# Scan loads of a hybrid encoder layer: keys stored by scan step, gate rows loaded once for each direction

## The chip, the cores and the metric

The kernel runs on one NeuronCore of a Trainium2 chip. The metric is the device time of one execution in microseconds, lower is better. One core has five engines that run side by side, each through its own list of instructions in order: TensorE (PE), VectorE (DVE), ScalarE (ACT), GpSimd (POOL) and SyncE (SP). SP computes nothing here: it issues the transfers between the chip's memory (HBM) and the core's SBUF. The core's 16 DMA engines carry them out.

## The reference

One encoder layer on 2,048 tokens of width 1,024, all in float32. Three head groups read the same normalised input; their outputs go through one projection and are added to the residual. Then come cross attention to 256 memory tokens and a squared-ReLU MLP.

```python
h = rmsnorm(x, norm_mix_w[l])
(na_q, ..., gd_b, gd_a) = jnp.split(h @ w_in[l], IN_OFFSETS, axis=-1)
y_na = neighbourhood_attention(na_q, na_k, na_v, na_rel_bias[l])      # 6 heads of 64
y_ml = mlstm_mixer(...)            # 4 heads of 64, forwards and backwards
y_gd = gated_deltanet_mixer(...)   # 6 heads of 64, forwards and backwards
x = x + jnp.concatenate([y_na, y_ml, y_gd], axis=-1) @ w_out[l]
x = x + memory_cross_attention(rmsnorm(x, norm_xa_w[l]), rmsnorm(mem, norm_mem_w[l]), ...)
h = rmsnorm(x, norm_ffn_w[l])
x = x + jnp.square(jax.nn.relu(h @ w_ff1[l])) @ w_ff2[l]
```

The two recurrent groups cut the tokens into 32 chunks of 64 and carry a 64 x 64 state from chunk to chunk, once forwards and once backwards:

```python
# gated DeltaNet, one direction, chunk by chunk
def step(state, xs):
    u_c, w_c, a_c, qd_c, ks_c, gl_c = xs
    v_new = u_c - jnp.einsum('bhld,bhde->bhle', w_c, state)
    o = jnp.einsum('bhld,bhde->bhle', qd_c, state) + jnp.einsum('bhls,bhse->bhle', a_c, v_new)
    state = state * jnp.exp(gl_c)[..., None, None] + jnp.einsum('bhld,bhle->bhde', ks_c, v_new)
    return state, o
# mLSTM, one direction: c_prev, n_prev, m_prev come from such a scan too
m_t = jnp.maximum(jnp.max(dmat, axis=-1), inter)
s_intra = jnp.einsum('bhnld,bhnsd->bhnls', q, k) * jnp.exp(dmat - m_t[..., None])
a_inter = jnp.exp(inter - m_t)
num = a_inter[..., None] * (q @ c_prev) + s_intra @ v
```

## The kernel before

`mix` does the first half of the layer in three passes, `tail` the rest. **Pass A** projects the DeltaNet inputs in four blocks of 512 tokens, makes the gates, and for each token tile of 128 (`gram`) forms the products of keys and queries; `inv` inverts the triangular matrices. All that the scans need is written to scratch tensors in HBM: the inverses `w_d`, query products and state keys `sc_d`, decayed keys `kb_d`, values `v_d`, convolved queries `gd_c`, decay rows `g_st`.

**Pass B** runs the two scans, `gdn_scan` and `ml_scan`, side by side, 16 steps each. A step `m` does forward tile `m` and backward tile `15 - m` together: the forward direction lies in partitions 0 to 63 and the backward one in 64 to 127 (`CH`; `SR` is the other half for the state rows). A step has two halves (`i`), one chunk of 64 tokens each. In a half of `gdn_scan` matmuls (L680) make the new values, a copy on DVE (forward) and one on ACT (backward) bring them from PSUM to SBUF (L682), matmuls (L687) update the state, and two copies (L690) bring that back, so that the next half can begin; L694 and L696 make the output. Between the scans' instructions stands one piece per step of a list called `rest`: projections (L108) that do not depend on the scans.

Each step's inputs are loaded one step ahead by `load(m + 1)`. Of `gdn_scan`: `wp`, `sc` (two buffers each), `kb`, `ge`, `qe` (one buffer each). ACT takes the exponential of `ge` (L650), POOL multiplies `qe` with it (L653), PE multiplies `kb` with `wp` (L661). Of `ml_scan`: `mr_` (`r` in the code) and `msc` (`sc`) with two buffers, and `mkq`, `mqe`, `me` (`e`), `mge` with one. DVE subtracts `me` (L850), POOL masks it (L851), ACT takes its exponential (L852), and POOL multiplies `mqe` with `mge` (L871). Four loads of a step serve both directions with one transfer: `kb` (L641), `ge` (L649), `me` (L848), `mge` (L849). Their source is a slice of the form `[m:32 - m:31 - 2 * m]` of a tensor whose direction and tile are taken as one dimension; it has two elements, and behind it come 64 rows. In `ge`, `me` and `mge` the 64 rows are one row of HBM, read 64 times (`broadcast_to([2, 64, ...])`).

**Pass C** does the neighbourhood attention and the outputs of all heads; `tail` the output projection, cross attention and MLP.

The order of the instructions on each engine is set ahead by the framework's scheduler, which works from its own model of durations and from priorities; SP's list of transfers is part of that order. A load waits until its buffer is free. Each transfer that SP issues also waits for one of eight semaphores (`DMAHW0` to `DMAHW7`), which are used in turn.

Of the kernel before, what the change touches and what calls it, by code (L numbers as in the profile page):

```python
# [49 lines left out]
class Trunk:  # L50
# [61 lines left out]
    def mix(self, late):  # L112

        tc, nc, I, dr = self.tc, self.nc, self.I, self.dr
        dt = lambda name, shape: dr.tile(shape, F32, name=name)
        self.y_d = [dt(f"y_d{b}", [8, P, 512]) for b in range(4)]
        self.gd_c = dt("gd_c", [9, P, T])
        self.gate_d = dt("gate_d", [5, P, T])
        self.ho_d = dt("ho_d", [16, P, 2, 640])
        self.mlc_d = dt("mlc_d", [16, P, 4, P])  # L120
        self.mlv_d = dt("mlv_d", [16, P, 4, 65])
        self.nac_d = dt("nac_d", [6, P, T])
        self.nav_d = dt("nav_d", [T, 384])
        self.g_row = dt("g_row", [16, 2, 2, 6, 64])
        self.sc_d = dt("sc_d", [2, 16, 2, 64, 2, 6, 64])
        self.kb_d = dt("kb_d", [2, 16, 64, 2, 6, 64])
        self.g_st = dt("g_st", [2, 16, 2, 6, 64])
        self.v_d = dt("v_d", [16, 2, 64, 6, 64])
        self.x_d = dt("x_d", [384, 64, 64])
        self.w_d = [[dt(f"w_d{d}{g}", [64, 12 * (b - a), 64]) for g, (a, b) in enumerate(GROUPS)] for d in range(2)]  # L130
        self.wt_d = [dt(f"wt_d{d}", [192, 32, 32]) for d in range(2)]
        with ExitStack() as big:
            self.c = big.enter_context(self.pool("mixc", 1))
            c = self.c
            self.ind2 = self.load_const("ind2", [P, 2])
            self.gmask = self.load_const("gmask", [P, 2, 64])
            self.egl = c.tile([P, 4, 2, 2, 4, 6], F32, name="egl")
            self.rr = c.tile([P, 16, 12], F32, name="rr")
            self.gcm = c.tile([P, 2, 16, 4], F32, name="gcm")
            self.gtm = c.tile([P, 2, 16, 4], F32, name="gtm")  # L140
            self.cm = c.tile([P, 2, 16, 4], F32, name="cm")
            self.cmx = c.tile([P, 2, 16, 4], F32, name="cmx")
            self.wxx = c.tile([P, 2, 16, 4], F32, name="wxx")
            self.emt = c.tile([P, 2, 16, 4], F32, name="emt")
            self.rs = c.tile([P, 16], F32, name="rs")
            self.rp = big.enter_context(self.pool("rest", 2))
            self.np = big.enter_context(self.pool("nin", 1))
            rest = chain(self.ml_in((3, 2)), self.na_kv((3, 2)), self.renorm((0, 1)), self.na_kv((0, 1)), self.na_q((0, 1)), *([self.gdn_z((0, 1))] if ZB else []))
            self.pass_a(rest)
            self.pass_b(rest)  # L150
            for _ in rest:
                pass
            self.pass_c(late)
# [264 lines left out]
    def gram(self, t):  # L418

        nc, pool = self.nc, self.tp  # L420
# [3 lines left out]
        e = pool.tile([P, 2, 6, 64], F32, name="gr")  # L424
# [49 lines left out]
        for d in range(2):  # L474
            sc = pool.tile([P, 3, 6, 64], F32, name="sc")
            V.tensor_tensor(out=byp(sc[:, 0]), in0=gv[:, :, :, 0:64], in1=byp(e[:, d]), op=ALU.mult)
            V.tensor_tensor(out=sc[:, 1], in0=heads(kt), in1=col(kst[:, d]), op=ALU.mult)
            V.tensor_tensor(out=sc[:, 2], in0=heads(kt), in1=col(self.eg[:, t, d]), op=ALU.mult)
            nc.sync.dma_start(out=self.sc_d[d, t].rearrange("c s a h l -> (c s) (a h l)"), in_=sc[:, 0:2].rearrange("p a h l -> p (a h l)"))
            for c2 in range(2):  # L480
                nc.sync.dma_start(out=self.kb_d[d, t, :, c2], in_=sc[64 * c2:64 * c2 + 64, 2])

    def inv(self, g, dirs, late=False):

# [140 lines left out]
    def gdn_scan(self, pool):  # L625
# [4 lines left out]
        nc, dr = self.nc, self.dr  # L630
        V, G = nc.vector, nc.gpsimd
        CH = (slice(0, 64), slice(64, 128))
        SR = (slice(64, 128), slice(0, 64))

        def load(m):
            wp = pool.tile([P, 2, 2, 6, 64], F32, name="wp")
            sc = pool.tile([P, 2, 2, 3, 6, 64], F32, name="sc")
            kb = pool.tile([P, 2, 6, 64], F32, name="kb", bufs=1)
            ge = pool.tile([P, 2, 6, 64], F32, name="ge", bufs=1)
            qe = pool.tile([P, 6, P], F32, name="qe", bufs=1)  # L640
            nc.sync.dma_start(out=kb.rearrange("p c h l -> p (c h l)"), in_=self.kb_d.rearrange("d t s c h l -> (d t) s (c h l)")[m:32 - m:31 - 2 * m])  # L641
            for d in range(2):
                t = m if d == 0 else 15 - m
                g = next(g for g, (a, b) in enumerate(GROUPS) if a <= t < b)
                nc.sync.dma_start(out=wp[CH[d], d].rearrange("p c h l -> p (c h) l"), in_=self.w_d[d][g][:, 12 * (t - GROUPS[g][0]):12 * (t - GROUPS[g][0]) + 12])
                nc.sync.dma_start(out=sc[CH[d], d, :, 0:2].rearrange("p c a h l -> p c (a h l)"), in_=self.sc_d[d, t].rearrange("c s a h l -> s c (a h l)"))
                nc.sync.dma_start(out=sc[CH[d], d, :, 2].rearrange("p c h l -> p c (h l)"), in_=self.v_d[t].rearrange("c s h l -> s c (h l)"))
                nc.sync.dma_start(out=qe[SR[d]], in_=self.gd_c[0:3, :, P * t:P * t + P].rearrange("c (h e) l -> e (c h) l", h=2))
            nc.sync.dma_start(out=ge.rearrange("p c h l -> p (c h l)"), in_=self.g_st.rearrange("d t c h l -> (d t) (c h l)")[15 - m:17 + m:2 * m + 1, None].broadcast_to([2, 64, 768]))  # L649
            nc.scalar.activation(out=ge, in_=ge, func=AF.Exp)  # L650
            for d in range(2):
                t = m if d == 0 else 15 - m
                G.tensor_tensor(out=sc[SR[d], d, :, 0], in0=qe[SR[d]].rearrange("p h (c l) -> p c h l", c=2), in1=ge[SR[d]], op=ALU.mult)  # L653
                V.tensor_tensor(out=sc[SR[d], d, :, 1], in0=self.ident[SR[d], None, None, SR[d]].broadcast_to([64, 2, 6, 64]),
                                in1=self.egl[SR[d], t // 4, :, d, t % 4, :, None].broadcast_to([64, 2, 6, 64]), op=ALU.mult)
            for i in range(2):
                ps = self.sps.tile([P, 512], F32, name="pss")
                for h in range(6):
                    for d in range(2):
                        c2 = i if d == 0 else 1 - i  # L660
                        nc.tensor.matmul(out=ps[SR[d], 64 * h:64 * h + 64], lhsT=kb[CH[d], c2, h], rhs=wp[CH[d], d, c2, h], start=True, stop=True)  # L661
                for d in range(2):
                    c2 = i if d == 0 else 1 - i
                    nc.scalar.copy(out=wp[SR[d], d, c2], in_=ps[SR[d], :384].rearrange("p (h x) -> p h x", x=64))
            return wp, sc

        cur = load(0)
        for d in range(2):
            V.memset(cur[1][SR[d], d, d, 2], 0.0)
        evac = (V.tensor_copy, nc.scalar.copy)  # L670
        for m in range(16):
            nxt = load(m + 1) if m < 15 else None
            o = pool.tile([P, 2, 384], F32, name="o", bufs=1)
            wp, sc = cur
# [147 lines left out]
    def ml_scan(self, pool):  # L822
        tc, nc, dr = self.tc, self.nc, self.dr
        V, G = nc.vector, nc.gpsimd
        CH = (slice(0, 64), slice(64, 128))
        SR = (slice(64, 128), slice(0, 64))
# [7 lines left out]
        def load(m):  # L834

            sc = pool.tile([P, 2, 2, 2, 4, 64], F32, name="msc")
            r = pool.tile([P, 2, 2, 4, 65], F32, name="mr_")
            qe = pool.tile([P, 4, P], F32, name="mqe", bufs=1)
            ge = pool.tile([P, 4, P], F32, name="mge", bufs=1)
            kq = pool.tile([P, 2, 4, P], F32, name="mkq", bufs=1)  # L840
            e = pool.tile([P, 2, 4, 64], F32, name="me", bufs=1)
            for d in range(2):
                t = m if d == 0 else 15 - m
                nc.sync.dma_start(out=kq[:, d], in_=self.mlc_d[t])
                nc.sync.dma_start(out=r[CH[d], d].rearrange("p c h x -> p c (h x)"), in_=self.mlv_d[t].rearrange("(c s) h x -> s c (h x)", c=2))
                for a in range(2):
                    nc.sync.dma_start(out=qe[SR[d], a::2], in_=self.mlc_d[t, CH[a], 0:2])
            nc.sync.dma_start(out=e.rearrange("p c h l -> p (c h l)"), in_=self.mx_row.rearrange("d t c h l -> (d t) (c h l)")[m:32 - m:31 - 2 * m, None].broadcast_to([2, 64, 512]))  # L848
            nc.sync.dma_start(out=ge.rearrange("p h l -> p (h l)"), in_=self.ai_row.rearrange("d t h c l -> (d t) (h c l)")[15 - m:17 + m:2 * m + 1, None].broadcast_to([2, 64, 512]))  # L849
            V.tensor_tensor(out=e, in0=self.cmx[:, :, m, :, None].broadcast_to([P, 2, 4, 64]), in1=e, op=ALU.subtract)  # L850
            G.tensor_tensor(out=e, in0=e, in1=gm[:, None, None, :].broadcast_to([P, 2, 4, 64]), op=ALU.add)  # L851
            nc.scalar.activation(out=e, in_=e, func=AF.Exp)  # L852
# [16 lines left out]
            for d in range(2):  # L869
                t = m if d == 0 else 15 - m  # L870
# [3 lines left out]
            return sc, r  # L874

        cur = load(0)
        for d in range(2):
            V.memset(cur[1][SR[d], d, d], 0.0)
        evac = (V.tensor_copy, nc.scalar.copy)
        for m in range(16):  # L880
            nxt = load(m + 1) if m < 15 else None
            o = pool.tile([P, 2, 4, 64], F32, name="mo", bufs=1)
            sc, r = cur
# [528 lines left out]
```

## Time and profile before

| | |
|---|---|
| median of 2 runs | 4136.92 us (4133.67 to 4140.17) |
| the profiled execution | 4121.6 us |
| its span | 4119.8 us |
| PE busy | 3509.9 us, 85% of the span |
| DVE / ACT / POOL busy | 1794.2 / 1153.4 / 1583.3 us |
| moved by DMA | 466.17 MB, mean 113 GB/s |

The span is what the profiler recorded from the first instruction to the last; the execution's own time has 1.8 us around it. A busy share is an average over passes with different limits, so it is read stage by stage. Pass A lasts until about 840 us of the span, pass B until about 1,620, pass C until about 2,000; the rest is the tail, in which PE is busy almost without a break.

### The profile page before, as it was taken

How to read it: one execution, taken by the hardware profiler on the slowest of the kernel's cores; microseconds unless marked ns; L12 is line 12 of the kernel's file. 1: busy time of each engine (PE TensorE's matmuls, PEld its weight loads, DVE VectorE, ACT ScalarE, POOL GpSimd, SP SyncE). 2: the span in 40 equal slices, each digit the busy share in tenths (PEclk: the TensorE clock that was granted, in tenths of full speed). 3: DMA queues.
4: the chain of work that ended last, by engine and by line, in shares of the span. 5: the costliest groups of instructions: out<-in, count | busy, mean ns of one | idle time of the engine just before them, and what ended most of it. 6: DMA issues, size and time to landing. Idle time of an engine off the chain costs nothing.

```text
span 4119.8 us, 54195 instructions
## 1 busy us (share of the span) xinstructions
PE 3509.9 (85%) x21392; PEld 2805.2 (68%) x21392; DVE 1794.2 (44%) x3257; ACT 1153.4 (28%) x2015; POOL 1583.3 (38%) x947
## 2 busy tenths in 40 slices
PE   5878788865445556988999999999999999999998
PEld 4656666644334445655888888778888877888887
DVE  7697885513334343555543434532222244222224
ACT  3223232211111122444443333422211243221123
POOL 4444443622223223322544534433333354333333
PEclk9888888877767778988999999999999999999999
DMA  4638567554444445567423333321111132111112
GB/s 129 190 108 185 143 162 180 133 131 118 115 122 133 130 135 178 169 191 220 138 92 128 98 121 133 116 72 44 47 47 51 52 107 85 44 46 47 52 52 87
DMA packets 388902, 466.17 MB, mean 113 GB/s; under 512 B 152408, under 2 KB 280872, under 8 KB 385576
## 3 DMA queue, kind: packets, MB, share of 16 engines
q1 hardware_dynamic: 385032, 450.65, 37.5%
q0 software_dynamic: 3616, 12.06, 0.9%
q8 instruction: 169, 2.77, 0.3%
q14 instruction: 85, 0.70, 0.1%
HBM read 360.01 MB, written 102.60 MB: 112 GB/s over the span
## 4 chain that ended last, share of the span: by engine, by line
PE 48%; issue 1%; DVE 1%; ACT 1%; DMA 0%; POOL 0%; SPq 0%; POOLq 0%; DVEq 0%; ACTq 0%
PE psg L108 28%; PE psa L108 19%; PE psa L1192 0%; DMA wraw<-in_w_ff 0%; DVE nh L1017 0%; PE psm L99 0%; ACT whi L999 0%; DVE ss L1028 0%; PE psm L88 0%; DMA out_y<-nh 0%; POOL wlo L1001 0%; DVE xb L1263 0%; ACT acta L1149 0%; ACT acta L1018 0%; DVE nh L1263 0%
## 5 line engine op out<-in xcount | busy, mean ns | idle before, releaser
L1001 POOL TENSOR_TENSOR wlo<-wraw,whi 128x1024 fp32r<-128x1024 f32 (+2 forms) x401 | 838.8, 2093 | 1346.5 <-ACT whi L999 1306.3
L108 PE MATMUL psg<-acta,whi 128*128 128x512 f32 x3008 | 981.5, 407 | 41.6 <-ACT pad L297 22.4
L108 PE MATMUL psg<-actb,whi 128*128 128x512 f32 (+2 forms) x2752 | 862.2, 394 | 34.4 <-ACT pad L297 19.9
L999 ACT CAST whi<-wraw 128x1024 fp32r<-128x1024 f32 (+2 forms) x417 | 373.5, 896 | 1219.2 <-PE psa L108 557.3
L108 PEld LDWEIGHTS psg<-acta,whi 128*128 128x128 f32 x3008 | 579.9, 195 | 179.2 <-ACT pad L297 25.2
L108 PE MATMUL psa<-ht,whi 128*128 128x512 f32 x2048 | 638.5, 395 | 0.7 <-ACT whi L999 0.7
L108 PEld LDWEIGHTS psg<-actb,whi 128*128 128x128 f32 (+1 forms) x2752 | 520.9, 194 | 150.8 <-ACT pad L297 21.1
L108 PE MATMUL psg<-acta,wlo 128*128 128x512 f32 x1504 | 607.5, 405 | 9.1 <-POOL wlo L1001 9.1
L108 PE MATMUL psg<-actb,wlo 128*128 128x512 f32 (+2 forms) x1376 | 542.2, 395 | 19.3 <-POOL wlo L1001 19.3
L108 PEld LDWEIGHTS psa<-ht,whi 128*128 128x128 f32 x2048 | 384.1, 188 | 95.3 <-ACT whi L999 1.6
L108 PE MATMUL psa<-ht,wlo 128*128 128x512 f32 x1024 | 401.0, 396 | 0.5 <-POOL wlo L1001 0.5
L1241 DVE TENSOR_TENSOR fr<-fr 128x512 f32<-128x512 f32 x128 | 167.9, 1312 | 497.1 <-ACT fr L1240 497.1
L1254 DVE TENSOR_TENSOR xb<-psa,xb 128x512 f32<-128x512 f32 x256 | 175.6, 691 | 476.6 <-PE psa L108 476.6
L108 PEld LDWEIGHTS psg<-acta,wlo 128*128 128x128 f32 x1504 | 292.6, 195 | 77.8 <-POOL wlo L1001 12.6
L108 PEld LDWEIGHTS psg<-actb,wlo 128*128 128x128 f32 (+1 forms) x1376 | 266.6, 194 | 77.4 <-POOL wlo L1001 23.6
L1244 POOL TENSOR_TENSOR ht<-fr,ht 128x512 fp32r<-128x512 f32 x128 | 169.1, 1321 | 248.3 <-ACT ht L1243 247.0
L108 PEld LDWEIGHTS psa<-ht,wlo 128*128 128x128 f32 x1024 | 192.2, 188 | 47.2 <-POOL wlo L1001 1.7
L310 DVE SCALAR_TENSOR_TENSOR acc<-pad,vecs,acc 128x512 f32<-128x512 f32 (+2 forms) x144 | 151.8, 1057 | 1.1
L1028 DVE TENSOR_TENSOR ss<-ss,sqt 128x512 f32<-128x512 f32 (+1 forms) x91 | 120.3, 1322 | 51.5 <-ACT sqt L1027 48.4
L850 DVE TENSOR_TENSOR me<-cmx,me 128x512 f32<-128x512 f32 x16 | 11.1, 692 | 282.0 <-DMA me<-mx_row 199.9
L1243 ACT CAST ht<-fr 128x512 fp32r<-128x512 f32 x128 | 79.4, 621 | 180.3 <-DVE fr L1241 180.2
L680 PE MATMUL pss<-sc,wp 128*64 128x64 f32 x768 | 40.6, 251 | 98.7 <-ACT sc L690 69.7
(376 smaller groups left out, 4100.4 us busy)
## 6 DMA issues: line engine op xcount, KB each, us to landing
wraw<-in_w_ff SPq DMA_DIRECT2D x72, 512.0 KB
wraw<-in_w_ff SPq DMA_DIRECT2D x144, 256.0 KB
wraw<-in_w_gd SPq DMA_DIRECT2D x36, 512.0 KB
xt<-in_xT SPq DMA_DIRECT2D x16, 1024.0 KB
wraw<-in_w_out SPq DMA_DIRECT2D x32, 512.0 KB
wraw<-in_w_xq SPq DMA_DIRECT2D x32, 512.0 KB
wraw<-in_w_xo SPq DMA_DIRECT2D x32, 512.0 KB
sc_d<-sc SPq DMA_DIRECT2D x32, 384.0 KB
```

Source lines behind the costliest of these rows:

```text
L108: nc.tensor.matmul(out=out, lhsT=a(k), rhs=b(k), start=(i == 0), stop=(i == n - 1))
L310: V.scalar_tensor_tensor(out=acc[:, :n], in0=pad[:, p0 + j:p0 + j + n], scalar=cw(j), in1=acc[:, :n], op0=ALU.mult, op1=ALU.add)
L680: nc.tensor.matmul(out=ps[CH[d], 64 * h:64 * h + 64], lhsT=wp[:, d, cc[d], h], rhs=sc[:, d, cc[d], 2, h], start=True, stop=True)
L850: V.tensor_tensor(out=e, in0=self.cmx[:, :, m, :, None].broadcast_to([P, 2, 4, 64]), in1=e, op=ALU.subtract)
L999: nc.scalar.copy(out=hi, in_=raw)
L1001: (lo_eng or nc.gpsimd).tensor_tensor(out=lo, in0=raw, in1=hi.bitcast(F32), op=ALU.subtract)
L1028: nc.vector.tensor_tensor(out=ss, in0=ss, in1=sq, op=ALU.add)
L1241: V.tensor_tensor(out=r, in0=r, in1=r, op=ALU.mult)
L1243: S.copy(out=ht[:, 0], in_=r)
L1244: G.tensor_tensor(out=ht[:, 1], in0=r, in1=ht[:, 0].bitcast(F32), op=ALU.subtract)
L1254: V.tensor_tensor(out=xs[nb][:, j], in0=ps, in1=xs[nb][:, j], op=ALU.add)
```

## The change

`kb_d` gets the scan step as its first dimension: the key of backward tile `t` is stored under step `15 - t`, so that a step's load takes the two directions as 128 rows that follow each other. The loads of `ge`, `me` and `mge` become two transfers each, one for each direction, with 64 rows of the one source row. The values are the same, and so are the bytes; a step issues three transfers more.

```diff
-        self.kb_d = dt("kb_d", [2, 16, 64, 2, 6, 64])
+        self.kb_d = dt("kb_d", [16, 2, 64, 2, 6, 64])
...
             for c2 in range(2):
-                nc.sync.dma_start(out=self.kb_d[d, t, :, c2], in_=sc[64 * c2:64 * c2 + 64, 2])
+                nc.sync.dma_start(out=self.kb_d[15 - t if d else t, d, :, c2], in_=sc[64 * c2:64 * c2 + 64, 2])
...
-            nc.sync.dma_start(out=kb.rearrange("p c h l -> p (c h l)"), in_=self.kb_d.rearrange("d t s c h l -> (d t) s (c h l)")[m:32 - m:31 - 2 * m])
+            nc.sync.dma_start(out=kb.rearrange("p c h l -> p (c h l)"), in_=self.kb_d[m].rearrange("d s c h l -> (d s) (c h l)"))
...
-            nc.sync.dma_start(out=ge.rearrange("p c h l -> p (c h l)"), in_=self.g_st.rearrange("d t c h l -> (d t) (c h l)")[15 - m:17 + m:2 * m + 1, None].broadcast_to([2, 64, 768]))
+            for d in range(2):
+                nc.sync.dma_start(out=ge[SR[d]], in_=self.g_st[1 - d, 15 - m if d else m][None].broadcast_to([64, 2, 6, 64]))
...
-            nc.sync.dma_start(out=e.rearrange("p c h l -> p (c h l)"), in_=self.mx_row.rearrange("d t c h l -> (d t) (c h l)")[m:32 - m:31 - 2 * m, None].broadcast_to([2, 64, 512]))
-            nc.sync.dma_start(out=ge.rearrange("p h l -> p (h l)"), in_=self.ai_row.rearrange("d t h c l -> (d t) (h c l)")[15 - m:17 + m:2 * m + 1, None].broadcast_to([2, 64, 512]))
+            for d in range(2):
+                t = m if d == 0 else 15 - m
+                nc.sync.dma_start(out=e[CH[d]], in_=self.mx_row[d, t][None].broadcast_to([64, 2, 4, 64]))
+                nc.sync.dma_start(out=ge[SR[d]].rearrange("p h l -> p (h l)"), in_=self.ai_row[1 - d, t].rearrange("h c l -> (h c l)")[None].broadcast_to([64, 512]))
```

The scheduler orders pass B anew. Its lists are the same on every engine up to the first loads of pass B. SP has 48 transfers more; from the second load of `kb` to the sixteenth there stand 20.6 transfers a step before and 23.7 now (289 and 332 rows over 14 steps). Line numbers of the changed kernel are one higher from L650 on and three higher from L850 on (`load` of `ml_scan` up to `mqe`: one).

On SP, in the loads of a middle step, before:

```order
L844 DMA mkq<-mlc_d 128x512 [waits DMAHW5_49,PE_49]
L844 DMA mkq<-mlc_d 128x512 [waits DMAHW6_49]
L847 DMA mqe<-mlc_d 64x2x128 [waits DMAHW7_49]
L848 DMA me<-mx_row 128x1x512 [waits DMAHW0_49,DVE_49]
L849 DMA mge<-ai_row 128x1x512 [waits DMAHW1_49]
L648 DMA qe<-gd_c 64x6x128 [waits DMAHW2_49,Pool_49]
L648 DMA qe<-gd_c 64x6x128 [waits DMAHW3_49]
L649 DMA ge<-g_st 128x1x768 [waits DMAHW4_49]
L588 DMA nav_d<-rv 128x4x128 [waits DMAHW5_49,DVE_49]
```

The same place of SP now (`L845` is `mkq`'s load, `L851` and `L852` those of `me` and `mge`, `L650` that of `ge`):

```order
L845 DMA mkq<-mlc_d 128x512 [waits DMAHW4_49,PE_49]
L845 DMA mkq<-mlc_d 128x512 [waits DMAHW5_49]
L851 DMA me<-mx_row 64x512 [waits DMAHW6_49,DVE_49]
L648 DMA qe<-gd_c 64x6x128 [waits DMAHW7_49,Pool_49]
L648 DMA qe<-gd_c 64x6x128 [waits DMAHW0_49]
L650 DMA ge<-g_st 64x768 [waits DMAHW1_49]
L650 DMA ge<-g_st 64x768 [waits DMAHW2_49]
L852 DMA mge<-ai_row 64x512 [waits DMAHW3_49]
L851 DMA me<-mx_row 64x512 [waits DMAHW4_49]
L852 DMA mge<-ai_row 64x512 [waits DMAHW5_49]
L588 DMA nav_d<-rv 128x4x128 [waits DMAHW6_49,DVE_49]
```

Three transfers of 128 rows became six of 64, the two halves of `me` lie five places apart, and the eight semaphores go round as before.

On ACT, in a middle step, before (`sc_8155` is the step that is scanned, `sc_8455` the next, `ge_8751` belongs to the loads of the one after that):

```order
L696 COPY o_8504<-pss_8535 64x384
L852 ACTIVATE me_8895<-me_8895 128x512
L682 COPY sc_8155<-pss_8550 64x384
L593 ACTIVATE rt_10226<-psg_10201 128x512
L650 ACTIVATE ge_8751<-ge_8751 128x768
L696 COPY o_8504<-pss_8580 64x384
L690 COPY sc_8455<-pss_8565 64x384
L664 COPY wp_8748<-pss_8768 64x384 x2
```

The same step of ACT now (`sc_8168` is the step that is scanned, `ge_8770` belongs to the loads of the one after the next):

```order
L665 COPY wp_8470<-pss_8506 64x384 x2
L683 COPY sc_8168<-pss_8522 64x384
L651 ACTIVATE ge_8770<-ge_8770 128x768
L691 COPY sc_8168<-pss_8537 64x384
L593 ACTIVATE rt_10260<-psg_10235 128x512
L896 COPY mr__8311<-psl_8673 64x260
L697 COPY o_8521<-pss_8552 64x384
L683 COPY sc_8168<-pss_8567 64x384
```

The exponential of `ge` stood behind the second half's first copy (L682) and in front of its last (L690); it now stands between the two copies of the first half (L683 and L691).

## Rows read from the trace of the kernel before

**Rows 1.** The page, part 2: busy tenths and clock in 40 equal slices.

```profile
PE   5878788865445556988999999999999999999998
PEclk9888888877767778988999999999999999999999
DMA  4638567554444445567423333321111132111112
```

**Rows 2.** Windows by stage: busy us (instructions) of PE, PEld, DVE, ACT, POOL; PEclk, DMA share, GB/s.

```profile
300.00:840.00 540.00, 444.35 (x3351) 351.97 (x3352) 383.19 (x856) 153.36 (x221) 245.60 (x146) 0.84 0.65 162
840.00:1620.00 780.00, 425.06 (x5624) 345.93 (x5622) 267.43 (x556) 139.69 (x270) 227.28 (x161) 0.75 0.45 126
1620.00:2000.00 380.00, 342.94 (x1976) 225.68 (x1977) 190.21 (x520) 155.99 (x399) 121.18 (x63) 0.90 0.62 196
```

**Rows 3.** Waits from 840 to 1,620 us: engine, line, releaser; us in total, times, longest.

```profile
ACT ge L650 <- DMA ge<-g_st: 241.4, 16, 22.6
...
DVE me L850 <- DMA me<-mx_row: 199.9, 15, 22.6
...
POOL msc L871 <- DMA mge<-ai_row: 67.0, 5, 35.1
```

**Rows 4.** Timeline of a middle step, from 1,100 us: start, us, engine, line, instruction, idle before.

```profile
1126.13 1.93 SPq L649 DMA_DIRECT2D ge<-g_st  x1
...
1132.16 0.52 SPq L848 DMA_DIRECT2D me<-mx_row  x1
1132.72 5.78 SPq L849 DMA_DIRECT2D mge<-ai_row  x1
...
1141.75 0.84 ACT L650 ACTIVATE ge<-ge 128x768 f32<-128x768 f32 x1 [15.62 <-DMA ge<-g_st]
...
1147.22 0.69 DVE L850 TENSOR_TENSOR me<-cmx,me 128x512 f32<-128x512 f32 x1 [18.88 <-DMA me<-mx_row]
1147.94 0.55 DVE L682 COPY sc<-pss 64x384 f32<-64x384 f32 x1
```

**Rows 5.** Windows of 2 us in the same step, columns as in rows 2.

```profile
1134.00:1136.00 2.00, 0.00 (x0) 0.00 (x0) 0.00 (x0) 0.00 (x0) 0.00 (x0) 0.50 0.13 52
1136.00:1138.00 2.00, 0.00 (x0) 0.00 (x0) 0.00 (x0) 0.00 (x0) 0.00 (x0) 0.50 0.12 49
```

**Rows 6.** Windows of 2 us from 840 to 1,620: first and last of three kinds.

```profile
840.00:842.00 2.00, 2.00 (x6) 1.63 (x5) 0.00 (x0) 0.01 (x1) 2.00 (x1) 0.50 0.90 249
842.00:844.00 2.00, 2.00 (x7) 1.57 (x6) 0.00 (x0) 0.00 (x0) 2.00 (x1) 0.69 0.16 25
...
856.00:858.00 2.00, 2.00 (x11) 1.64 (x10) 0.00 (x0) 0.00 (x0) 0.50 (x1) 1.00 0.12 45
...
1572.00:1574.00 2.00, 0.00 (x0) 0.00 (x0) 0.80 (x2) 0.00 (x0) 0.06 (x1) 0.50 0.13 51
...
1612.00:1614.00 2.00, 0.27 (x3) 0.07 (x1) 1.88 (x9) 1.18 (x2) 1.24 (x2) 1.00 0.29 96
...
1618.00:1620.00 2.00, 0.00 (x0) 0.00 (x0) 0.00 (x0) 0.00 (x0) 1.10 (x1) 0.50 0.89 358
```

**Rows 7.** Timeline of DVE: the copy that ends a half step of the DeltaNet scan (L690).

```profile
943.77 0.56 DVE L690 COPY sc<-pss 64x384 f32<-64x384 f32 x1
...
1152.00 0.56 DVE L690 COPY sc<-pss 64x384 f32<-64x384 f32 x1 [1.26 <-PE pss L687]
...
1166.33 0.56 DVE L690 COPY sc<-pss 64x384 f32<-64x384 f32 x1 [1.06 <-PE pss L687]
...
1193.09 0.56 DVE L690 COPY sc<-pss 64x384 f32<-64x384 f32 x1
...
1593.12 0.56 DVE L690 COPY sc<-pss 64x384 f32<-64x384 f32 x1 [3.01 <-PE pss L687]
```

**Rows 8.** Timeline of pass A: a 64-row broadcast of one row is issued (L426) and used (L445).

```profile
666.79 0.49 SPq L426 DMA_DIRECT2D gr<-g_row  x1
...
669.99 0.96 DVE L445 TENSOR_TENSOR gr<-gr,gcg 128x768 f32<-128x768 f32 x1 [6.62 <-DMA gr<-g_row]
```

## The prediction

> **What bounds the kernel now.** I read the slices first: PE is busy 0.8 or more of most of the span, but from about 840 to 1,620 us it falls to 0.4 to 0.6, and the granted clock falls with it [rows 1]. The windows by stage say how much is at stake there: in pass B PE is busy for 425 of 780 us at a clock of 0.75, and the DMA engines, at 0.45 and 126 GB/s, do less than in the stages on either side, 0.65 and 0.62 [rows 2]. So neither PE nor the sum of the transfers bounds pass B; something waits. (The chain of waits, followed back from the end, stops in the tail and says nothing of pass B.)
>
> The waits of the stage name it: ACT waits 241 us for `ge`, all 16 times, DVE 200 us for `me`, POOL 67 us for `mge` [rows 3]. These are three of the four transfers whose source has a first dimension of two. One step shows how they hold the rest: SP is done with issuing `ge` at 1128.1, `me` is out at 1132.7, and issuing `mge` takes 5.8 us; ACT, idle for 15.6 us, gets `ge` at 1141.75, and DVE, idle for 18.9 us, gets `me` at 1147.22. Right behind `me` on DVE stands the scan's own copy L682, so the scan stands still too [rows 4]. In those microseconds no engine computes at all, and the DMA engines show a share of 0.13 and about 50 GB/s [rows 5]. 0.13 of 16 engines is two engines, running all the time, while 14 have nothing.
>
> How much of pass B is like that? I cut its 780 us into 390 windows of 2 us and sorted them by DMA share; the first and last of each kind stand in [rows 6]. 116 windows lie between 0.11 and 0.15 (two engines alone; mean 49 GB/s, PE busy 0.26), 74 between 0.16 and 0.40 (mean 0.27), 180 above 0.40 (mean 0.79 and 206 GB/s, PE busy 0.68), and 20 below 0.11.
>
> **The change part by part.** *Held time.* The pure windows are 116 x 2 = 232 us. The 74 mixed ones, 148 us, have a mean of 0.27 between 0.13 and 0.79, so about (0.79 - 0.27) / (0.79 - 0.13) = 0.79 of them, 117 us, is the same state. Together 349 us in which two engines carry a backlog. Its bytes must still go: 349 us x 49 GB/s = 17.1 MB, which at the 206 GB/s of the open windows takes 83 us. If the new forms spread over all engines, pass B loses 349 - 83 = 266 us.
>
> A second way, from the scan's steps. The copies L690 on DVE run from 943.77 to 1593.12, 31 of them: 15 steps of 43.3 us [rows 7]. Their distances alternate: a half without a held load took 14.3 us (1152.00 to 1166.33), the next, with one in it, 26.8 us (to 1193.09). With two halves of 14.3 us a step is 28.6, and 15 steps save 15 x 14.7 = 220 us. The head of the stage, 840 to 944, has 17 pure and 10 mixed windows of the above: 34 + 16 = 50 us held, less its bytes 38 us. Together 258 us. I take **260 us** from the two.
>
> *What must fit into the rest.* PE was busy for a quarter of the held windows, some 60 us; the 180 open windows have 0.32 x 360 = 115 us of idle PE, which hides it; without that cover it would cost the 60. The transfers: 780 us x 126 GB/s = 98.3 MB. At the 196 GB/s of the stage after, that takes 501 us, at the 162 GB/s of the stage before, 607 [rows 2]; my 520 us asks for 189. It is nearer the first, because the windows without held transfers in this very stage reach 206.
>
> *Three more transfers a step.* 48 issues of 0.52 us [rows 4] are 25 us of SP's time. A step's 23.7 issues make 12 to 14 us of 28, so SP hides them; if SP were the bound they would cost 25. What waits behind them on SP are the step's later loads and the stores of `rest`.
>
> *`kb`.* The stores are as many, with the same rows at other addresses: nothing. The load has 128 rows of its own behind each other instead of two times 64; its share of the gain is in the held time.
>
> *The new order.* ACT's exponential of `ge` moves forward, between the two copies of the first half. That adds a wait: behind it on ACT stand L691 and all later copies of the backward direction, and PE's next half waits for those. On SP the next step's `sc` loads stand ahead of this `ge`, and they wait for the buffer that the scan frees as the step begins; four of them, two of `mr_`, `kb`, two of `qe` and two of `ge` are 11 issues of about 0.55 us, so `ge` is out 6 us into the step and, landing like the nearest row, a spread broadcast that DVE had 3.2 us after its issue [rows 8], is there after some 10. The scan needs ACT for L691 after about 4. That is 0 to 6 us a step, 0 to 90 us in 15. I take 0, since the 14.3 us of a half already hold several such waits, and keep the 90 for the range. Next late after `ge` and `me` are then the `sc` loads, which wait for the scan itself, and PE's `rest`.
>
> A rule speaks against the split. The rows show gr, loaded in two halves, waited for only briefly [rows 8]. The Trainium skill (DMA: Bandwidth & Descriptors, section Rules for kernel authors) advises against two transfers to disjoint partition halves, as both use the same 16 engines and serialize. By it the halves of `ge`, `me` and `mge` would gain nothing; no row here has one load both whole and in halves.
>
> **The sum.** Profiled execution 4121.6 - 260 = 3861.6 us. The median shown, 4136.9, lies 15.3 us above that execution; the changed kernel should lie as far above its own, so **3877 us**. A difference under 2% (83 us) I count as no change, about what a measurement of this kernel can tell.
>
> **The rivals.** *The transfers become the bound* at the rate of pass A: pass B takes 607 us, 173 less, 3964 us. For it: the same small rows from HBM and SP's one queue; against: the open windows' 206 GB/s.
>
> *The gain is partly eaten by the order*: the 90 us of ACT's wait come in full, 3967 us, with the 25 us of issues 3992. For it: SP's list, on which `ge` cannot be out earlier; against: PE has `rest` to do meanwhile.
>
> *It does not do what it says*: the two halves of a load go one after the other on the same few engines, as the rule above would have it, and nothing is gained but 25 us of issues: 4162 us. For it: the held share of 0.13 could belong to the 64-fold reading of one HBM row and not to the first dimension. Against: gr is read so too, and arrives in 3.2 us.
>
> *Slower*: that same reading of one row sets the time to land, and `ge` still takes 13.7 us from issue to use (1128.06 to 1141.75 [rows 4]). SP's transfers wait in turn for eight semaphores, so each of the 3.1 more a step costs 13.7 / 8 = 1.7 us when landing is what SP waits for: 5.3 us a step, 85 us in 16, 4222 us. It decides from a landing of about 13.7 us on; below that it stays within 2%.
>
> **How the numbers follow.** Forecast 0.71, the transfers as bound 0.14, the order 0.08, no gain 0.04, slower 0.03. The first three are all faster by over 2%: 0.93; same 0.04; slower 0.03. For the low end the held bytes find their room in the windows that are open already: 360 us at 0.79 leave 0.21 x 360 = 76 us of all 16 engines, nearly the 83; then pass B loses 349 - 7 = 342 us, 3795. The high end is the order with its issues, 3992. That leaves out the last two cases and the far ends of the others, some 0.2.
>
> **What would show it.** In the profile after, the 2 us windows of pass B with a share near 0.13 and idle engines should be nearly gone (under 15 of 116), the stage should end near 1,360 instead of 1,620, with a DMA share near 0.65 and some 190 GB/s, and ACT's wait for `ge` should fall from 241 us to under 60. The L690 copies should come every 14 us or so, without the alternation, and PE's clock in the stage should rise above 0.75. All before 840 us should look the same. If ACT still waits about 6 us for `ge` in each step, the order ate part; if the windows at 0.13 stay, the first dimension was not what held the engines, and the prediction is wrong; if the windows go but the stage does not shorten, the loads were hidden behind something that I did not see.

## The result, and the profile after

The changed kernel takes 3812.95 us (median of 2 runs, 3803.89 to 3822.01) against 4136.92: the ratio is 0.9217 with a 95% interval of 0.9118 to 0.9316, so it is faster by 324 us. The profiled execution has a span of 3802.1 us, 317.7 less than before.

The page's slices of the changed kernel, part 2, to be held against [rows 1]: the dip of PE and of its clock between 840 and 1,620 us is gone, and the DMA engines are busiest in the very place where they were half idle.

```profile
PE   6878778798888799999999999999999999999998
PEclk9888878889899898899999999999999999999999
DMA  4647574758888657653343233111111141111112
```

Windows by stage of the changed kernel, columns as in [rows 2]: a stretch of pass A, the 15 middle steps of pass B, and pass C.

```profile
300.00:840.00 540.00, 442.63 (x3331) 350.65 (x3330) 379.12 (x853) 151.28 (x220) 247.07 (x144) 0.84 0.65 161
...
903.00:1282.00 379.00, 317.64 (x4943) 258.18 (x4945) 251.03 (x488) 117.00 (x232) 196.61 (x140) 0.94 0.84 215
...
1305.00:1690.00 385.00, 356.55 (x2072) 238.95 (x2073) 191.79 (x533) 161.51 (x408) 127.56 (x68) 0.91 0.63 197
```

Pass A reads as before, 0.65 and 161 GB/s; in pass B the share rose from 0.45 to 0.84 and the rate from 126 to 215 GB/s, PE is busy 0.84 of the time at a clock of 0.94. From the first issue of `kb` to the last issue of `ho_d` from `mo`, pass B lasted 772.6 us before (843.5 to 1616.1) and lasts 464.9 now (845.4 to 1310.3). That is 308 of the 318 us.

The waits of pass B in the changed kernel, the same three as in [rows 3]:

```profile
ACT ge L651 <- DMA ge<-g_st: 88.4, 16, 9.3
...
DVE me L853 <- DMA me<-mx_row: 40.2, 14, 4.0
...
POOL msc L874 <- DMA mge<-ai_row: 5.0, 2, 2.7
```

Windows of 2 us, as in [rows 6], of 840 to 1,300 us: of 230 windows 3 lie between 0.11 and 0.15, all with PE busy throughout, in place of 116 of 390; 192 lie above 0.40, and their mean is 0.97 and 247 GB/s. The first and last of the 192:

```profile
840.00:842.00 2.00, 1.14 (x26) 0.98 (x23) 0.00 (x0) 1.98 (x2) 0.38 (x1) 1.00 0.80 287
...
1298.00:1300.00 2.00, 0.00 (x0) 0.00 (x0) 1.85 (x7) 0.00 (x0) 1.70 (x2) 0.50 1.04 386
```

The line L691 (L690 before), DVE's copy that ends a half step: count, shortest, median and longest in ns, first and last start in us.

```profile
L691 DVE COPY sc<-pss x31: 553/561/562, 902.8 to 1281.8; 64x384 f32<-64x384 f32 x31
```

15 steps in 379.0 us are 25.3 us a step, where [rows 7] gave 43.3. This pair of starts is the measure for pass B in the experiments: divided by 15, it is free of the head and the end of the stage. The changed kernel profiled once more (e12) gave 25.5.

### The profile page after: what moved, and what is told of

It reads as the page before. It is cut to its first block, busy times and chain, and to the rows that moved or that the text cites. A ratio compares the mean times of both kernels' runs of the same rounds, so it can differ in the third digit from the quotient of the medians.

```text
span 3802.1 us, 54291 instructions
## 1 busy us (share of the span) xinstructions
PE 3473.0 (91%) x21392; PEld 2774.0 (73%) x21392; DVE 1799.1 (47%) x3257; ACT 1152.7 (30%) x2015; POOL 1593.9 (42%) x947
## 4 chain that ended last, share of the span: by engine, by line
PE 52%; DVE 1%; ACT 1%; issue 1%; DMA 0%; POOL 0%; POOLq 0%; DVEq 0%; SPq 0%; ACTq 0%
PE psg L108 31%; PE psa L108 21%; PE psa L1195 0%; PE psm L88 0%; DVE nh L1020 0%; DVE ss L1031 0%; PE psm L99 0%; DMA out_y<-nh 0%; ACT whi L1002 0%; POOL wlo L1004 0%; DMA xb<-x_d 0%; DVE xb L1266 0%; ACT acta L1152 0%; ACT acta L1021 0%; ACT sqt L1030 0%
## 5 line engine op out<-in xcount | busy, mean ns | idle before, releaser
L1243 ACT ACTIVATE fr<-psg 128x512 f32<-128x512 f32 x128 | 75.9, 593 | 132.1 <-PE psg L108 132.1
L503 DVE TENSOR_TENSOR tv<-x 96x30 f32<-96x30 f32 (+37 forms) x210 | 89.4, 442 | 10.7 <-DMA x<-x_d 9.7
```

What stands on the lines that cost most here:

```text
L503: V.tensor_tensor(out=tv, in0=m[:, j + 1:32, j:j + 1].broadcast_to([2 * N, n, j]), in1=m[:, j:j + 1, 0:j].broadcast_to([2 * N, n, j]), op= ...
L1243: S.activation(out=r, in_=ps, func=AF.Relu)
```

## The experiments

Theory A says: a source whose first dimension is two puts the whole transfer on two of the 16 DMA engines; these two then have more to do than the other 14, every other transfer has a share on them too, and a step lasts as long as the busiest engine works. Theory B, the rival: what costs is that ACT, DVE and POOL wait for `ge`, `me` and `mge`, rows of HBM that are read 64 times; `kb`, for which the stage's list of waits has one wait of PE of 4.8 us, is then worth nothing.

### Each part alone

Four kernels between before and after, each one or two hunks of the change on top of the kernel before.

```diff
# e1: the two kb_d hunks and kb's load alone     # e2: ge, me, mge split, kb as before
# e3: ge split alone                             # e4: me and mge split alone
```

> The kernel before with kb alone stored by step (one load of 128 rows). Theory A (a first dimension of two puts a load on two engines, and pass B runs at the pace of these two): kb's 384 KB are 8 us a step of the pair's time at 49 GB/s and 1.6 us when spread, so some 6 us of a step of 48 go: about 95 us faster, 4040 us, although hardly anyone waits for kb. Theory B (what costs is the wait of ACT, DVE and POOL for the broadcasts of one row): kb is no broadcast, 4125 to 4137 us.

> The kernel before with ge, me and mge split by direction, kb as it was. Theory A: kb still runs on two engines, so about 95 us of the gain are missing, 3910 us. Theory B: the broadcasts were all of it, 3815 to 3830 us.

> The kernel before with ge alone split. Theory A: as many bytes as kb, as much gain, about 95 us, 4040 us. Theory B: the largest single wait of the stage (241 of some 510 us of waits for the three) goes, about 150 us, 3985 us.

> The kernel before with me and mge split, ge and kb as they were. Theory A: 512 KB leave the pair, 10.7 us a step less 2.1, about 126 us, 4010 us; the gains of e1, e3 and e4 add up to that of the change (324 us). Theory B: about 160 us, 3975 us.

The kernel before took 4130.5 us beside them. e1: 4028.1, ratio 0.9743 (0.9712 to 0.9774), 102 us faster. e2: 3927.8, 0.9504 (0.9468 to 0.9540), 203 us. e3: 4025.4, 0.9737 (0.9694 to 0.9780), 105 us. e4: 4042.7, 0.9784 (0.9742 to 0.9826), 88 us; the interval of e4 reaches past 0.98, so a gain of over 2% is not shown for it. The copy at the end of a half step in e1, e2, e3 and e4:

```profile
L690 DVE COPY sc<-pss x31: 553/560/563, 928.8 to 1492.0; 64x384 f32<-64x384 f32 x31
```

```profile
L691 DVE COPY sc<-pss x31: 553/560/564, 914.4 to 1384.4; 64x384 f32<-64x384 f32 x31
```

```profile
L691 DVE COPY sc<-pss x31: 553/560/561, 929.8 to 1517.4; 64x384 f32<-64x384 f32 x31
```

```profile
L690 DVE COPY sc<-pss x31: 556/561/563, 941.8 to 1521.8; 64x384 f32<-64x384 f32 x31
```

The steps are 37.5, 31.3, 39.2 and 38.7 us (before 43.3, after 25.3). Theory B falls with e1: `kb`, for which hardly anyone was seen to wait, is worth 102 us by itself, as much as `ge`, for which ACT waited 241 us. And e2, in which the three broadcasts are spread, keeps 31.3 us a step with `kb` alone in the old form. The windows of 2 us say the same: between the first issue of `kb` and the last of `ho_d`, 116 lay between 0.11 and 0.15 before, 74 do in e1, 52 in e3, 58 in e4, 19 in e2 and 3 in the changed kernel. Each load that gets the new form takes part of the stretches on two engines away. The waits of pass B in e1 show how that works: `ge` and `me` are still waited for, for less time, as they must be by theory A, in which the two engines reach them sooner.

```profile
ACT ge L650 <- DMA ge<-g_st: 196.3, 16, 20.3
DVE me L850 <- DMA me<-mx_row: 191.2, 16, 67.9
```

(The 67.9 us of `me` are the wait of the first step, which the list of the kernel before puts down to another transfer; without it, 123.3 us in 15 waits stand against 199.9 in 15 there.) So the load that a wait is named after did not alone make it: `kb` shortened the waits for the two others. Not as expected: e4 gained 88 and not 126 us, and the three parts alone add up to 295 of 324 us. A step has 18.0 us less in the whole change and 5.7 + 4.1 + 4.6 = 14.5 less in the parts, so the parts bring more together than apart (`kb` 6.1 us from e2 to the change, 5.7 in e1). Why `me` and `mge`, with 4/3 of `kb`'s bytes, bring less than `kb` was not tried apart.

### The first dimension by itself

If the number of engines is what the first dimension sets, 4 and 8 must lie between 2 and 128. `kb_d` gets gaps, so that the groups of a load's rows can't be taken together:

```diff
-        self.kb_d = dt("kb_d", [16, 2, 64, 2, 6, 64])
+        self.kb_d = dt("kb_d", [16, 4, 33, 2, 6, 64])       # e6: [16, 8, 17, 2, 6, 64]
...
+                for q in range(2):
+                    nc.sync.dma_start(out=self.kb_d[15 - t if d else t, 2 * d + q, 0:32, c2], in_=sc[64 * c2 + 32 * q:64 * c2 + 32 * q + 32, 2])
...
+ in_=self.kb_d[m, :, 0:32].rearrange("d s c h l -> d s (c h l)")
```

> The changed kernel with kb stored in four groups of 32 rows with a gap of one row between them, so that its load has a first dimension of 4 (the store of a key becomes two stores of 32 rows, which falls in pass A; pass B alone is compared, from the first issue of kb to the last of ho_d from mo, 465 us in the changed kernel). Theory A (the first dimension is the number of engines): 96 KB on each of four engines are 3.9 us a step in place of 1.6: pass B longer by 20 to 40 us. If any first dimension but two is spread: as the changed kernel, 465.

> As before, but eight groups of 16 rows, a first dimension of 8 (four stores in place of one in pass A). Theory A: 48 KB on each of eight engines, 2.0 us in place of 1.6: pass B longer by 0 to 12 us. Rival: 465.

The copies L692 of e5 and e6:

```profile
L692 DVE COPY sc<-pss x31: 553/561/562, 962.4 to 1402.0; 64x384 f32<-64x384 f32 x31
```

```profile
L692 DVE COPY sc<-pss x31: 553/560/562, 976.7 to 1381.2; 64x384 f32<-64x384 f32 x31
```

29.3 and 27.0 us a step, from one execution each. The same bytes of `kb` thus cost, above the spread form, 6.1 us a step with a first dimension of 2 (e2), 4.0 with 4, 1.7 with 8. The order is theory A's; the expectation had put 2.3 and 0.4 for the last two, so the cost falls more slowly than the engines' share of bytes. The measure that had been laid down, the length of pass B, missed as well: 561.0 us in e5 and 496.1 in e6 against 464.9, 96 and 31 us longer where theory A had put 20 to 40 and 0 to 12. Of these, 61 and 26 us lie in the 15 middle steps; in e5 the head of the stage grew too (88.9 us from the first issue of `kb` to the first copy, 57.4 in the changed kernel). The rival, 465 us for both, falls; why the price is above theory A's stays open. The more stores make pass A longer (the first `kb` is issued at 873.5 and 919.8 us, not at 845.4), so their whole times, 3900.2 and 3916.4 us, say nothing of the load.

### Does the number of transfers cost?

```diff
+                for q in range(2):
+                    o = SR[d].start + 32 * q
+                    nc.sync.dma_start(out=ge[o:o + 32], in_=self.g_st[1 - d, 15 - m if d else m][None].broadcast_to([32, 2, 6, 64]))
# me and mge likewise
```

> The changed kernel with each piece of ge, me and mge cut once more, into 32 rows: six transfers a step more, same bytes. If SP's issues or the eight semaphores now set the pace of pass B: 96 issues of 0.52 us or more, 50 us slower, 3863. If the bytes on the 16 engines set it: within 12 us of the changed kernel.

3808.9 us against 4138.1, ratio 0.9214 (0.9186 to 0.9242); the changed kernel, timed again in a later comparison (e12), 0.9226 (0.9198 to 0.9255). Its copies:

```profile
L693 DVE COPY sc<-pss x31: 556/561/564, 905.9 to 1289.7; 64x384 f32<-64x384 f32 x31
```

25.6 us a step, 0.3 more than the changed kernel and 0.1 more than e12. 96 further issues cost nothing that shows.

### What bounds pass B now?

e9 keeps the first step's rows of `ge` and `mge` and takes those of `mge` for `me`, so that its output is not the layer's; e8, the same with the rows in two buffers of their own, needed more of SBUF than is left and has no time. e10, e11 and e13 do the 64-fold copying on PE instead of in the transfers; e12 is the changed kernel on the same chip as e9 to e11; e13 ran on another.

```diff
# e9
-            for d in range(2):
+            if m == 0:   # ge, mge; me's rows are mge's
...
# e10: ge; e13: me in the same way (psl, 512 columns, DVE subtracts from PSUM); e11: both
+                nc.sync.dma_start(out=ge[64 - 64 * d:65 - 64 * d], in_=self.g_st[1 - d, 15 - m if d else m][None])
+            for c in range(2):
+                ps = self.sps.tile([P, 512], F32, name="pss")
+                for o in (0, 64):
+                    nc.tensor.matmul(out=ps[o:o + 64, :384], lhsT=self.ones[o:o + 1].broadcast_to([1, 64]), rhs=ge[o:o + 1, c], start=True, stop=True)
+                nc.scalar.activation(out=ge[:, c], in_=ps[:, :384].rearrange("p (h l) -> p h l", l=64), func=AF.Exp)
```

> The changed kernel with ge (and its exponential) and mge loaded in the first step alone and used in all, and mge's rows in the place of me's (so the later steps compute with wrong rows). 896 KB of 6.1 MB a step are left out, with six transfers and one ACT instruction. If pass B is now bound by the 16 engines at some 247 GB/s: 3.6 us a step, some 55 us faster than the changed kernel, 3758. If it is bound by the scan's own chain, by PE or by the transfers' number: within 15 us of it.

> The changed kernel with ge's two rows loaded once each (3 KB) and spread over the 64 partitions by matmuls with a column of ones; ACT's exponential then reads PSUM in two pieces. 378 KB a step less by DMA, four matmuls of 384 columns and one ACT instruction more. If the engines' bytes bound pass B: 1.5 us a step less, 15 to 25 us faster than the changed kernel. If PE, at 0.84 busy in the stage, is as near: 0 to 10 us slower.

> As before, and me in the same way (two matmuls of 512 columns, DVE subtracts from PSUM): 630 KB a step less by DMA. If the bytes bound pass B: 2.5 us a step less, 25 to 40 us faster than the changed kernel. If PE or the two PSUM buffers of the mLSTM scan bound it: 0 to 20 us slower.

> The changed kernel itself, on the same chip as the three above, for comparison: 0.922 of the kernel before.

> The changed kernel with me alone spread by matmuls (two of 512 columns), ge as in the changed kernel. 252 KB a step less by DMA. If the gain of e11 (55 us on the changed kernel) came from me alone, since me reaches DVE sooner: 35 to 55 us faster than the changed kernel, 0.909 to 0.914 of the kernel before. If it takes both, because only both together take enough bytes off the engines: within 15 us of the changed kernel, 0.919 to 0.926.

Beside a kernel before of 4142.1 us (e13: 4129.9): e9 3776.9, ratio 0.9132 (0.9096 to 0.9168); e10 3835.0, 0.9267 (0.9243 to 0.9290); e11 3760.4, 0.9091 (0.9068 to 0.9114); e12 3815.5, 0.9226 (0.9198 to 0.9255); e13 3842.1, 0.9299 (0.9283 to 0.9315). The copies of e9, e10, e11 and e13:

```profile
L696 DVE COPY sc<-pss x31: 553/560/563, 899.7 to 1240.3; 64x384 f32<-64x384 f32 x31
```

```profile
L695 DVE COPY sc<-pss x31: 553/560/561, 902.7 to 1293.2; 64x384 f32<-64x384 f32 x31
```

```profile
L695 DVE COPY sc<-pss x31: 558/561/562, 892.7 to 1244.1; 64x384 f32<-64x384 f32 x31
```

```profile
L691 DVE COPY sc<-pss x31: 554/560/563, 907.8 to 1331.2; 64x384 f32<-64x384 f32 x31
```

Steps of 22.7, 26.0, 23.4 and 28.2 us. The middle steps in windows, e9 first, then e10, e11 and (to 1,300 us) e13:

```profile
900.00:1240.00 340.00, 305.55 (x4914) 249.38 (x4911) 249.30 (x494) 107.22 (x218) 195.60 (x139) 0.95 0.76 197
```

```profile
903.00:1293.00 390.00, 340.82 (x5032) 261.59 (x5032) 227.52 (x509) 119.25 (x245) 179.59 (x137) 0.89 0.72 189
```

```profile
893.00:1244.00 351.00, 342.37 (x5173) 253.77 (x5170) 250.52 (x508) 124.65 (x249) 177.62 (x139) 0.99 0.79 206
```

```profile
903.00:1300.00 397.00, 343.32 (x4857) 270.29 (x4855) 246.54 (x489) 122.32 (x230) 202.18 (x138) 0.90 0.77 202
```

In e9 15% of the bytes gone bring 2.6 us a step and some 39 us in all, 0.7 of what pure transfer time would be and between its two expectations: the share falls to 0.76 while PE rises to 0.90. That would fit a stage bound by the bytes of all 16 engines with PE close behind, but it does not show it, because e9 has no wait for the rows left either. The lists of waits of the middle steps, in the changed kernel (two lines), in e10 and in e13:

```profile
ACT ge L651 <- DMA ge<-g_st: 67.4, 13, 6.6
DVE me L853 <- DMA me<-mx_row: 40.2, 14, 4.0
```

```profile
DVE me L857 <- DMA me<-mx_row: 74.9, 14, 10.1
```

```profile
ACT ge L651 <- DMA ge<-g_st: 73.5, 12, 9.0
```

Where both waits are gone (e9 and e11), a step takes 22.7 and 23.4 us; where one is left, it has grown, and a step takes 26.0 and 28.2, although both kernels move fewer bytes than the changed one. So e9's gain can be that of the bytes or that of the waits, and what bounds the changed kernel's pass B is not shown. For e11 it is plainer: PE is busy 342 of 351 us at a clock of 0.99, and pass B is PE's. It is the fastest kernel here, faster than the changed one by 0.9226 - 0.9091, 1.35% of the kernel before, with intervals that lie apart.

e10 and e13, either half of e11, are both slower than the changed kernel, by 20 and some 30 us (0.0073 of the kernel before; e13 has no changed kernel beside it on its chip). For e10 the second expectation had allowed 10 us; for e13 neither had one. They lose in different places. In the profiled execution of e13 pass B lasts 508.3 us in place of 464.9, and what follows it is as long as in the changed kernel (2496.8 and 2491.8 us). In that of e10 pass B is 12 us shorter, 453.0 us (its first expectation had put 15 to 25 for the whole); what follows takes 2543.5 us, and part of it runs at a lower clock. From 1,500 to 1,700 us in e10, then in the changed kernel:

```profile
1500.00:1700.00 200.00, 174.93 (x909) 109.95 (x909) 93.88 (x265) 73.74 (x193) 54.74 (x35) 0.75 0.60 185
```

```profile
1500.00:1700.00 200.00, 185.78 (x1076) 126.43 (x1074) 105.45 (x262) 89.25 (x212) 69.41 (x42) 0.88 0.58 180
```

So e10 as a whole says little of what bounds pass B. Each edit lets the scheduler order the kernel anew, and no run holds the order fixed, so whether the order or the matmuls' place in the chain makes e10 and e13 slower stays open.

## Why the prediction was right, point by point

**The reading of the profile** held in each step. The stage that the slices pointed to gave 308 of the 318 us; the windows at 0.13 were what the change removed; pass A is as it was, and what follows pass B is shorter by 12 us (2503.7 and 2491.8). That two engines were the cause was only argued from 0.13 = 2/16. The runs show it: `kb`, no broadcast and hardly waited for, is worth 102 us (e1), and its cost falls with the first dimension, 6.1, 4.0, 1.7 us a step for 2, 4 and 8 (e2, e5, e6). The Trainium skill states such a rule (DMA: Bandwidth & Descriptors, section Why a DMA increments its semaphore by 16 and not by 1): the number of engines is the largest number up to 16 that divides, on both sides, the size of the slowest dimension that is not 1. The runs agree with the order of the four forms, 6.1, 4.0, 1.7 and 0 us; that the cost at 4 and 8 is larger than the bytes make it, the rule doesn't tell.

**The size was short**, 260 us against 308 in pass B. The term that was mis-sized is the price of the held bytes, "which at the 206 GB/s of the open windows takes 83 us". The windows of held time are nearly gone (3 of the pure ones and 13 of the mixed), so by that sum 349 - 308 = 41 us came back. The windows above 0.40 before were no measure of free engines: in the changed kernel such windows run at 0.97 and 247 GB/s, and in e2, with `kb` alone left in the old form, at 0.82 and 214. Theory A would explain that, as every spread transfer has a share on the two late engines; no run shows it by itself. 17.1 MB at 247 are 69 us, 14 of the 42 us that were too much; the other 28 I can't place, and the share of the mixed windows was only interpolated. The second way failed at the same place: the half of 14.3 us, taken from one pair as free of held loads, became 12.6 on the mean (25.3 / 2), which is 15 x 3.3 = 50 us; the head of the stage gave 43 where 38 was put (first copy at 902.8 instead of 943.8, the stage's start 2 us later), and its end, from the last copy on, took 5.5 us more.

A sum by the busiest engine fits the kernel before. Its middle steps, for which this is the row, move 125 GB/s x 649 us / 15 = 5.41 MB each:

```profile
944.00:1593.00 649.00, 345.68 (x4920) 282.49 (x4922) 242.66 (x499) 115.78 (x230) 188.01 (x139) 0.74 0.45 125
```

Of these 1.31 MB on two engines at 49 GB/s together are 26.7 us, and the other 4.10 MB on all at 247 GB/s 16.6 us: 43.3 us, as measured. After, 5.43 MB at 247 are 22.0, where a middle step takes 25.3, so 3.3 us a step are something else than bytes. The rate of 247 shows only in the changed kernel, so the sum could not have been made ahead. For the parts it gives 6.4 us for `kb` and for `ge` (5.7 and 4.1 measured) and 8.6 for `me` and `mge` (4.6): it has the two last as the largest part, and they are not.

**Three more transfers a step** at nothing: no run adds these alone, but six more on top cost nothing that shows (e7).

**The new order's wait** was there, and in the size that was kept for the range: ACT still waits 88.4 us for `ge`, 16 times, of which 67.4 in the middle steps, where under 60 had been foretold. That is 5.5 us a step, the sign that the prediction had named for an order that eats part of the gain. On the timeline of the changed kernel the wait stands in front of ACT's output copy L697 and its first half's copy L683:

```profile
1056.00 0.84 ACT L651 ACTIVATE ge<-ge 128x768 f32<-128x768 f32 x1 [5.23 <-DMA ge<-g_st]
1056.74 0.46 ACT L697 COPY o<-pss 64x384 f32<-64x384 f32 x1
...
1057.23 0.56 DVE L697 COPY o<-pss 64x384 f32<-64x384 f32 x1 [4.70 <-ACT o L697]
...
1058.45 0.55 DVE L683 COPY sc<-pss 64x384 f32<-64x384 f32 x1
...
1059.04 0.47 ACT L683 COPY sc<-pss 64x384 f32<-64x384 f32 x1 [1.07 <-DVE sc L683]
```

DVE's L697 waited 4.70 us for ACT's, which stood behind `ge`, and the scan's own copy L683 stood behind it on DVE; the matmuls that it copies had ended at 1054.2. In 8 of the 13 middle waits `ge` stands right in front of ACT's L691, as here:

```profile
1234.41 0.56 DVE L691 COPY sc<-pss 64x384 f32<-64x384 f32 x1
...
1239.80 0.84 ACT L651 ACTIVATE ge<-ge 128x768 f32<-128x768 f32 x1 [6.46 <-DMA ge<-g_st]
1240.67 0.47 ACT L691 COPY sc<-pss 64x384 f32<-64x384 f32 x1
```

The backward copy comes 6.3 us after the forward one, and the next half's matmuls of that direction (L681, from 1241.19) had to wait for it; PE filled most of that time with projections. So the wait lies on the scan's path, as the prediction had described it, and the 0 that it took for the price is not borne out. What it costs no run tested by itself: e9 and e11, in which it is gone, have steps shorter by 2.6 and 1.9 us, but they differ in more than that. The gain came out larger than forecast even so; whatever the order cost, the held time gave that much more than the 308 us.

**The rivals.** The transfers come nearer to being the bound (a share of 0.84), but at 215 GB/s and not at the 162 of that rival's price. The case in which the split gains nothing falls with e3: `ge`, its row still read 64 times for each direction, gains 105 us by the split alone, so the 64-fold reading was not what held the two engines. The Trainium skill's rule that was weighed against the split (DMA: Bandwidth & Descriptors, section Rules for kernel authors) gives as its reason that both halves use all 16 engines. The runs agree where a load does so already: cutting the halves into quarters gained nothing (e7). The prediction read [rows 8] as a short wait for `gr`; the row has DVE idle for 6.6 us before it, and only the 3.2 us from issue to use are short. The slower case, 4222 us, did not come: the kernel is 324 us faster.

**What had been foretold of the profile:** windows at 0.13 under 15, there are 3; the stage's end near 1,360, it is 1,310; a share of 0.65 and 190 GB/s, they are 0.84 and 215 in the middle steps; copies every 14 us without alternation, they come every 12.6 on the mean, but from 8.1 to 18.2 apart, with long and short halves still in turn for much of the stage; a clock above 0.75, it is 0.94.

## What to carry to other kernels

A DMA share that stands still at a small multiple of 1/16 while all engines wait (0.13 here) is a reason to suspect that a few DMA engines carry a backlog; look for transfers whose outermost dimension is small, and not only for those that an engine is seen to wait for: `kb`, with one wait of 4.8 us, was worth 102 us. Lay data out so that the rows of one load follow each other, or cut the load so that each piece has 64 rows in front; here 96 more issues cost nothing that shows (e7). When sizing such a gain, do not take the rate of the windows in between (206 GB/s) as the rate that the engines will reach once the backlog is gone (247). And when a new order puts a wait in front of a copy that a recurrence needs, look at what stands behind it on that engine before its price is put at nothing.

## What the runs showed of the hardware that was not expected

The last transfer to get the new form was worth as much as when it was the first, or more (`kb`: 6.1 us a step after the other three, 5.7 alone), and a first dimension of 8 still cost 1.7 us a step for one transfer of 384 KB (one execution). Two changes that each made the kernel slower than the changed one (0.9267 and 0.9299 against 0.9226) made it faster together (0.9091).
